# A two-layer hybrid attention trunk on one Trainium2 core: the seven products of a Strassen-Winograd projection in another order, with the loads and epilogues around them moved

## Chip, cores and metric

The kernel runs on one core of one Trainium2 chip. The metric is device microseconds (us) from the first to the last instruction of one execution; the time shown is the median of several runs.

## The reference, cut to what matters

The input x (512 frames of 2048 channels, fp32) gets 16 meta tokens in front: L = 528 positions. One layer of gated differential attention and one layer of gated sliding-window attention follow, then a final norm. The change lies in the first layer:

```python
h = rms_norm(x, norm_g)
q, k, v, gate = jnp.split(h @ w_in, 4, axis=-1)      # w_in: 2048 x 8192
q = partial_rope(q.reshape(B, L, 16, 128), cos, sin)
k = partial_rope(k.reshape(B, L, 16, 128), cos, sin)
...
o = diff_attention(q, k, v, lam, cid)                # 8 heads, block-causal softmax
o = rms_norm(o, subln_g) * (1.0 - lambda_init)
o = o.reshape(B, L, D_MODEL) * jax.nn.silu(gate)
return x + o @ w_out
```

## The kernel before, in words

All tiles hold channels in partitions and positions along the free dimension. fp32 matmuls run as sums of three products of rounded halves: an operand is split into hi (a rounded copy, made by ScalarE) and lo (the rest, made by VectorE), and hi x hi, hi x lo and lo x hi are added in PSUM. `wsplit` (L89) splits a 128 x 1024 weight piece (512 KB), `split4` (L161) a piece of x, scaled by the norm's gain g, which lies in the tile `vec`.

**The projection `h @ w_in`** is made for 64 output tiles of 128 channels, in 32 pairs (`Pair`, L312). Pairs 0 to 2 are plain (`plain`, L387): 192 matmuls of 264 columns each. The other 29 use Strassen-Winograd's scheme on 2 x 2 blocks (two tiles, two halves of the input channels, two halves T of the positions): seven products of 24 matmuls each. `build_forms` (L271) makes the seven right-hand forms f1 to f7 of x once; their left-hand forms are sums of four weight pieces: a, b and d are loaded by SP, and s1 and s3 are loaded by SP and then added to by a second DMA that GpSimd (POOL) issues with accumulation (L326). `ORDER` (L341) is the order of the products, `BANK` (L342) the PSUM tile that each adds into: B (two buffers), C and D (one each). `product` (L360) issues one product and its epilogue: a copy by ScalarE where a group is read for the first time, an addition by VectorE after that. A group that is read and then added to further has to wait for that read. The pair's two results e[0] (tags e0x and e0y in turn) and e[1] (one buffer, tag e1) go on to `finish` (L729): rope or the scale rstd for q and k, then a store to DRAM that POOL issues (L464, L468); for the gate pairs 24 to 31 `finish_gate` (L695): scale, tanh, two products with th and with the attention output read back from DRAM (L705), and a store (L708).

**Attention** of head h is a generator, `heads_attend` (L530), that `tick` advances between the passes of the products by about 0.67 steps a product. `v_rows` (L470) loads one half of a head's v from DRAM (`ldv`, issued on ScalarE's queue, L472) and transposes it on TensorE (tile `Tv`); it runs twice a head. `pv` (L608) multiplies the weights with v.

**The start** (L420 to L430): `x_in` loads x by channel tiles and splits them, `w_in` loads and splits the first four weight pieces, `SumSq` (L228) sums the squares of x for the norm: ScalarE squares, POOL adds. `norm_a` (L256) makes rstd.

**The end of the projection**: `og_in` (L719) loads the gated outputs back (`ldog`) and splits them into og0 to og3, the operands of the out-projection, which begins at 882 us.

The order of each engine's instructions is set by a scheduler (from the order in the text, `tc.high_priority()`, the pools' buffers, and its own model); every engine and every DMA queue then runs its row in that order.

Of the kernel before, what the change touches and what calls it, by code (L numbers as in the profile page):

```python
# [14 lines left out]
D = 2048  # L15
# [28 lines left out]
def trunk(tc, xT, w, vecs, sinks, rope, ident_in, out):  # L44
# [58 lines left out]
    def wunit(m, half, place=None, urgent=True):  # L103

        with tc.high_priority() if urgent else ExitStack():
            raw = wp.tile([128, 1024], F32, tag=f"raw{raws[0] % 3}", name="raw")
            raws[0] += 1
            nc.sync.dma_start(raw, w[m, half])
            return wsplit(raw, place)
# [118 lines left out]
    class SumSq:  # L228


        def __init__(self, n, part, spare):
# [13 lines left out]
    ssx = SumSq(  # L245
        L, lambda i: etmp(("e0y", "rr")[i], f"ssx{i}"), lambda k: ld.tile([128, L], F32, tag="ld", name="sqx")
    )
# [64 lines left out]
    class Pair:  # L312


        def __init__(self, m):
            self.m, self.wr = m, {}
# [24 lines left out]
    ORDER = (1, 5, 6, 2, 7, 3, 4)  # L341
    BANK = {1: "B", 6: "B", 7: "B", 4: "B", 5: "C", 3: "C", 2: "D"}  # L342
# [17 lines left out]
    def product(p, i):  # L360
# [3 lines left out]
        if i in (1, 5, 2):  # L364
            setattr(p, b, bank(b))
        o = getattr(p, b)
        passes(o, x, i, i in (1, 5, 2), True)
# [5 lines left out]
        elif i == 6:  # L373
            act.activation(p.e[0][:, t1], o, AF.Copy, scale=-1.0)  # L374
        elif i == 2:
            add(p.e[0][:, t0])
# [10 lines left out]
    def plain(p, units):  # L387

        for t in range(2):
            o = [bank("B"), bank("BCD"[t + 1])] if t == 0 else [bank("B"), bank("D")]  # L390
# [15 lines left out]
            else:  # L406
                p.e[1] = etmp("e1", "e1")
# [7 lines left out]
    def w_in(t, half):  # L415
        place, tag = Q.get([128, 2, 1024], F32R, f"wu{t}{half}")
        units[t, half] = wunit(t, half, place, False)
# [35 lines left out]
    def finish_qk(p, h, i0):  # L453

        for i, t in enumerate(p.e):
            if i0 + i == 0:
                r = etmp("rr", "rr")
                dve.stream_shuffle(out=r, in_=t, mask=[(j + 16) % 32 for j in range(32)])
                dve.tensor_tensor(out=t, in0=t, in1=CR, op=ALU.mult)
                dve.tensor_tensor(out=r, in0=r, in1=SR, op=ALU.mult)  # L460
                dve.tensor_tensor(out=t, in0=t, in1=r, op=ALU.add)
            else:
                dve.tensor_tensor(out=t, in0=t, in1=rstd, op=ALU.mult)
            pl.dma_start(qkv_dram[h][128 * (i0 + i) : 128 * (i0 + i) + 128], t)  # L464

    def finish_v(p, h):
        for i, t in enumerate(p.e):
            pl.dma_start(qkv_dram[h][512 + 128 * i : 640 + 128 * i], t)  # L468

    def v_rows(h, dt, vq):  # L470
        raw = ld.tile([128, L], F32, tag="ld", name="ldv")
        nc.scalar.dma_start(raw, qkv_dram[h][512 + 128 * dt : 640 + 128 * dt])  # L472
        T = psT.tile([128, 512], F32, tag="T", name="Tv")
# [56 lines left out]
    def heads_attend(h):  # L530
# [98 lines left out]
        if tails:  # L629
            tails.pop()()  # L630
            yield
        v_rows(h, 0, vq)
# [4 lines left out]
        v_rows(h, 1, vq)  # L637
# [5 lines left out]
        pv(0)  # L643
# [3 lines left out]
        yield  # L647
        trows(2)
        yield
# [6 lines left out]
        for _ in pre:  # L656
            yield
        trows(3)
        tmeta(1)
        yield  # L660
        pv(1)
# [33 lines left out]
    def finish_gate(p, j):  # L695
# [3 lines left out]
        for i, z in enumerate(p.e):  # L699
            dve.tensor_tensor(out=z, in0=z, in1=rstd, op=ALU.mult)  # L700
            th = etmp("rr", "th")
            act.activation(th, z, AF.Tanh, scale=0.5)
            dve.scalar_tensor_tensor(out=z, in0=th, scalar=1.0, in1=z, op0=ALU.add, op1=ALU.mult)
            oo = ld.tile([128, L], F32, tag="ld", name="ldo")
            pl.dma_start(oo, o_dram[j][i])  # L705
            pl.tensor_tensor(out=z, in0=z, in1=oo, op=ALU.mult)
            if j < 7:
                pl.dma_start(og_dram[j][i], z)  # L708
            else:
                split_og(14 + i, z)  # L710
# [7 lines left out]

    def og_in(q4):  # L719
# [4 lines left out]
        for m in range(4 * q4, min(4 * q4 + 4, 14)):  # L724
            t = ld.tile([128, L], F32, tag="ld", name="ldog")
            pl.dma_start(t, og_dram[m // 2][m % 2])
            split_og(m, t)

    def finish(j):  # L729
        p = PAIRS[j]  # L730
        made[0] = j + 1
        if j >= 24:
            finish_gate(p, j - 24)
        elif j % 3 < 2:
            finish_qk(p, j // 3, 2 * (j % 3))
        else:
            finish_v(p, j // 3)
            steps.append(heads_attend(j // 3))

    for j in range(PLAIN):  # L740
        plain(PAIRS[j], units if j == 0 else {})
        if j == 0:
            PAIRS[PLAIN].load("s1", "s3")
            Q.free(*wtags)
            building = build_forms()
            for _ in range(5):
                next(building)
            steps.append(building)
            rate[:] = [1.0, 0.0]
        finish(j)  # L750
# [7 lines left out]
    for j in range(PLAIN, 32):  # L758
        p, q = PAIRS[j], PAIRS[j + 1] if j < 31 else None
        if j == 28:  # L760
            drain()
            og_in(0)
        for i in ORDER:
            product(p, i)
# [278 lines left out]
    m = 0  # L1043
# [146 lines left out]
```

## Time and profile before

| | us |
|---|---|
| median of 3 runs (lowest, highest) | 1748.71 (1746.19, 1749.03) |
| the profiled execution, its own time | 1755.2 |
| its span, first to last instruction | 1753.4 |
| busy TensorE (PE), share of the span | 1665.7, 95% |
| busy VectorE (DVE), ScalarE (ACT), GpSimd (POOL) | 1132.1, 866.4, 237.2 |

The span has four stretches: 0 to 96 us, loading and the plain pairs; 96 to 675 us, the pairs of q, k and v with attention between their products; 675 to 882 us, the gate pairs; 882 to 1753 us, everything after the projection (out-projection, second layer), where the text of the kernel is the same before and after. "Busy" of PE counts a matmul from its start to its modelled end; a wait is put down to what released the engine last. The granted clock (PEclk) is 1.00 at 2.4 GHz and 0.50 at 1.2 GHz.

### The profile page before, as it was taken

What the parts mean: (1) busy time and instruction counts of PE and PEld (TensorE: products, weight loads), DVE (VectorE), ACT (ScalarE), POOL (GpSimd) and SP (SyncE); (2) the same over time, 40 slices, a digit from 0 to 9 for tenths busy, and PEclk for the clock granted to TensorE, in tenths of its full rate; (3) what the DMA queues carried; (4) which work ended last, traced back from release to release, by engine and by line L of the source; (5) the groups of instructions that cost most, each with busy time, mean ns of one, the idle gap of its engine ahead of it and who ended that gap; (6) DMA issues with size and microseconds to landing.
All of it is one profiled execution on the core that took longest, in us unless ns stands there. A gap on an engine that the chain in (4) does not pass through costs nothing.

```text
span 1753.4 us, 28723 instructions
## 1 busy us (share of the span) xinstructions
PE 1665.7 (95%) x11383; PEld 1544.2 (88%) x11383; DVE 1132.1 (65%) x1667; ACT 866.4 (49%) x1628; POOL 237.2 (14%) x260
## 2 busy tenths in 40 slices
PE   7899998989999989988899999999999999999996
PEld 7899998989999989988899999888887788888886
DVE  6976777777778767776633337566677777762234
ACT  8565655656566656543522324344545554553331
POOL 3211111111111102243211100010000000000111
PEclk9999999999999999999999999999999999999998
DMA  7367566766676676685644445321222222233332
GB/s 249 113 184 196 161 181 178 189 174 185 186 204 187 169 202 171 182 252 171 209 134 132 141 129 158 131 96 62 84 65 80 73 72 73 69 107 119 120 126 96
DMA packets 83494, 254.81 MB, mean 145 GB/s; under 512 B 10400, under 2 KB 14624, under 8 KB 83360
## 3 DMA queue, kind: packets, MB, share of 16 engines
q1 hardware_dynamic: 47616, 161.25, 27.5%
q0 software_dynamic: 16992, 59.62, 14.8%
q10 hardware_dynamic: 18752, 32.12, 5.9%
q8 instruction: 89, 1.46, 0.3%
q14 instruction: 45, 0.37, 0.1%
HBM read 223.34 MB, written 29.61 MB: 144 GB/s over the span
## 4 chain that ended last, share of the span: by engine, by line
PE 73%; DMA 10%; DVE 8%; ACT 4%; issue 4%; POOL 1%; ACTq 0%; DVEq 0%; SPq 0%; POOLq 0%
PE acc L141 40%; PE B L354 12%; PE C L354 6%; DMA ldv<-qkv_dram 3%; DVE wlo L98 2%; DMA ldqk<-qkv_dram 2%; PE D L354 2%; PE po L616 2%; PE TB L196 1%; PE B L397 1%; DMA ldog<-og_dram 1%; PE poB L983 1%; PE acct L1102 1%; DMA qkv_dram<-e 1%; DMA og_dram<-e 1%
## 5 line engine op out<-in xcount | busy, mean ns | idle before, releaser
L98 DVE TENSOR_TENSOR wlo<-raw,whi 128x1024 fp32r<-128x1024 f32 x140 | 173.7, 1241 | 239.6 <-PE acc L141 187.0
L96 ACT ACTIVATE whi<-raw 128x1024 fp32r<-128x1024 f32 x140 | 148.3, 1060 | 229.0 <-PE acc L141 192.0
L141 PE MATMUL acc<-hh,whi 128*128 128x512 f32 x512 | 202.6, 396 | 0.0
L141 PE MATMUL acc<-hl,whi 128*128 128x512 f32 x512 | 201.0, 392 | 0.0
L141 PE MATMUL acc<-hh,wlo 128*128 128x512 f32 x512 | 129.5, 393 | 0.0
L141 PEld LDWEIGHTS acc<-hh,wlo 128*128 128x128 f32 x512 | 95.9, 188 | 21.8
L141 PEld LDWEIGHTS acc<-hh,whi 128*128 128x128 f32 x512 | 96.3, 188 | 21.1
L141 PEld LDWEIGHTS acc<-hl,whi 128*128 128x128 f32 x512 | 96.4, 188 | 20.5
L326 POOL DMA_DIRECT2D rs<-in_w x58 | 51.9, 894 | 339.8 <-DMA rs<-in_w 166.8
L96 ACT ACTIVATE whi<-rb 128x1024 fp32r<-128x1024 f32 x58 | 61.4, 1059 | 72.4 <-PE B L354 35.8
L243 POOL TENSOR_TENSOR ss<-ss,sq 128x528 f32<-128x528 f32 (+1 forms) x26 | 35.0, 1346 | 445.1 <-ACT sq L242 445.1
L96 ACT ACTIVATE whi<-ra 128x1024 fp32r<-128x1024 f32 x58 | 61.4, 1059 | 58.5 <-PE B L354 29.5
L946 ACT ACTIVATE p<-SB,nm 128x208 f32<-128x208 f32 (+2 forms) x128 | 51.3, 412 | 68.4 <-DVE es L943 61.1
L98 DVE TENSOR_TENSOR wlo<-rb,whi 128x1024 fp32r<-128x1024 f32 x58 | 71.9, 1240 | 16.6 <-PE C L354 8.6
L98 DVE TENSOR_TENSOR wlo<-rs,whi 128x1024 fp32r<-128x1024 f32 x58 | 72.9, 1257 | 9.1 <-PE B L354 6.3
L96 ACT ACTIVATE whi<-rs 128x1024 fp32r<-128x1024 f32 x58 | 61.3, 1056 | 34.7 <-PE C L354 30.9
L354 PE MATMUL C<-f3h,whi 128*128 128x264 f32 x232 | 60.6, 293 | 6.9 <-ACT e L379 6.9
L885 POOL TENSOR_TENSOR qr<-qr,SR 128x512 f32<-128x512 f32 x16 | 22.2, 1390 | 331.7 <-DVE qr L884 264.3
L354 PE MATMUL B<-f7h,whi 128*128 128x264 f32 x232 | 60.1, 293 | 6.0 <-ACT e L374 5.7
L354 PE MATMUL B<-f4h,whi 128*128 128x264 f32 x232 | 64.1, 307 | 0.2
L100 DVE SCALAR_TENSOR_TENSOR wlo<-ra,whi 128x1024 fp32r<-128x1024 f32 x29 | 36.2, 1247 | 42.0 <-PE C L354 29.1
L354 PE MATMUL C<-f5h,whi 128*128 128x264 f32 x232 | 59.7, 291 | 2.9 <-DVE e L369 2.9
(455 smaller groups left out, 5163.0 us busy)
## 6 DMA issues: line engine op xcount, KB each, us to landing
raw<-in_w SPq DMA_DIRECT2D x148, 512.0 KB, 3.3
rs<-in_w SPq DMA_DIRECT2D x58, 512.0 KB, 4.3
rs<-in_w POOLq DMA_DIRECT2D x58, 512.0 KB, 5.8
ra<-in_w SPq DMA_DIRECT2D x29, 512.0 KB, 4.5
rb<-in_w SPq DMA_DIRECT2D x29, 512.0 KB, 4.3
rd<-in_w SPq DMA_DIRECT2D x29, 512.0 KB, 5.7
qkv_dram<-e POOLq DMA_DIRECT2D x48, 264.0 KB, 2.8
hr<-h_dram ACTq DMA_DIRECT2D x32, 256.0 KB, 3.3
```

Of the source, the lines that this page charges most:

```text
L96: act.activation(hi, raw, AF.Copy, scale=sign)
L98: dve.tensor_tensor(out=lo, in0=raw, in1=f(hi), op=ALU.subtract)
L100: dve.scalar_tensor_tensor(out=lo, in0=raw, scalar=sign, in1=f(hi), op0=ALU.mult, op1=ALU.subtract)
L141: pe.matmul(acc[:, s, 0:n], lhsT=a[:, ws], rhs=b[kt // 4][:, kt % 4, c0 : c0 + n], start=(kt == 0 and a is whi and b is hi), stop=(kt == K ...
L196: pe.transpose(o, i, ident[0 : i.shape[0], 0 : i.shape[0]])
L243: pl.tensor_tensor(out=self.acc[i], in0=self.acc[i], in1=t, op=ALU.add)
L326: pl.dma_start(t, w[self.m + 1, 1 if n == "s1" else 0], accum_op=ALU.add)
L354: pe.matmul(o, lhsT=a[:, ws], rhs=b[:, k, :], start=(first and k == 0 and b is fh[i] and a is hi), stop=(last and k == 7 and a is lo), ski ...
L397: pe.matmul(o[s], lhsT=a[:, ws], rhs=b[:, k8, :], start=(half == 0 and k8 == 0 and a is x[0] and b is fh[i]), stop=(half == 1 and k8 == 7 ...
L616: pe.matmul(pov[:, dt, c0:256], lhsT=v_, rhs=w_[:, j, c0:256], start=(j == 0 and k == 0), stop=False)
L885: pl.tensor_tensor(out=r, in0=r, in1=SR[:, META:], op=ALU.mult)
L946: act.activation(p[:, rt, 0:W], Sv[:, rt, :], AF.Exp, bias=nm[:, rt : rt + 1], accum_out=s[:, rt : rt + 1])
```

## The change

The products are issued in the order 1, 5, 2, 6, 3, 4, 7. The fourth starts a PSUM group of its own in D, so that the seventh, now last, adds one result to both halves of e[1]. Each result is finished by itself, e[0] after product 3 and e[1] after product 7. Loads of v are issued one step before their transposes. Gate pairs keep z and the product apart, prefetch the attention output, and the gated outputs are read back into the five places of `po5` some products before they are split. x's loads are issued with high priority, so are the first weight pieces; the adds of x's squares move to VectorE, and the norm (`norm_a`) moves from the first steps of `build_forms` into the second plain pair.

```diff
-    def wunit(m, half, place=None, urgent=True):
+    def wunit(m, half, place=None, raw=None):
-        with tc.high_priority() if urgent else ExitStack():
-            raw = wp.tile([128, 1024], F32, tag=f"raw{raws[0] % 3}", name="raw")
+        with tc.high_priority():
+            if raw is None:
+                raw = wp.tile([128, 1024], F32, tag=f"raw{raws[0] % 3}", name="raw")
...
                 act.activation(t, src, AF.Square)
-                pl.tensor_tensor(out=self.acc[i], in0=self.acc[i], in1=t, op=ALU.add)
+                self.engine.tensor_tensor(out=self.acc[i], in0=self.acc[i], in1=t, op=ALU.add)
...
-            nc.sync.dma_start(x, xT[kt])
+            with tc.high_priority():
+                nc.sync.dma_start(x, xT[kt])
...
-            if kt % 4 == 3:
-                yield
-        norm_a()
-        yield
...
-    ORDER = (1, 5, 6, 2, 7, 3, 4)
-    BANK = {1: "B", 6: "B", 7: "B", 4: "B", 5: "C", 3: "C", 2: "D"}
+    ORDER = (1, 5, 2, 6, 3, 4, 7)
+    BANK = {1: "B", 6: "B", 7: "B", 5: "C", 3: "C", 2: "D", 4: "D"}
...
-        if i in (1, 5, 2):
+        if i in (1, 5, 2, 4):
             setattr(p, b, bank(b))
         o = getattr(p, b)
-        passes(o, x, i, i in (1, 5, 2), True)
+        passes(o, x, i, i in (1, 5, 2, 4), True)
...
-        elif i == 7:
-            add(p.e[1][:, t1])
...
         elif i == 4:
             act.activation(p.e[1][:, t0], o, AF.Copy)
+        else:
+            e = two(p.e[1])
+            dve.tensor_tensor(out=e, in0=o.unsqueeze(1).to_broadcast([128, 2, HALF]), in1=e, op=ALU.add)
...
-        v_rows(h, 0, vq)
+        raw = v_in(h, 0)
         yield
         yield from srows(1)
         trows(0)
         yield
-        v_rows(h, 1, vq)
+        v_rows(raw, 0, vq)
+        raw = v_in(h, 1)
         yield
         trows(1)
         tmeta(0)
         yield from srows(2)
         yield
-        pv(0)
+        v_rows(raw, 1, vq)
         yield
         r3 = srows(3)
         next(r3)
         yield
+        pv(0)
+        yield
...
-            oo = ld.tile([128, L], F32, tag="ld", name="ldo")
-            pl.dma_start(oo, o_dram[j][i])
-            pl.tensor_tensor(out=z, in0=z, in1=oo, op=ALU.mult)
-            if j < 7:
-                pl.dma_start(og_dram[j][i], z)
+        pl.tensor_tensor(out=o, in0=z, in1=o, op=ALU.mult)
+        if j < 7:
+            pl.dma_start(og_dram[j][i], o)
...
+    def og_load(*ms):
+        for m in ms:
+            pl.dma_start(po5[:, m % 5, :], og_dram[m // 2][m % 2])
...
         for i in ORDER:
+            if i == 2 and not steps:
+                gate_in(p, j - 24, 0)
+                gate_in(p, j - 24, 1)
             product(p, i)
+            if i in (3, 7):
+                finish(j, i // 7)
+            if i == 7 and j == 27:
+                drain()
+            elif i == 6 and j == 28:
+                og_load(0, 1, 2, 3)
+            elif i == 6 and j == 29:
+                og_in(0)
+            elif i == 6 and j == 30:
+                og_load(4, 5, 6, 7, 8)
             if q:
-                q.load(*{2: ("a",), 5: ("s1",), 7: ("s3",), 3: ("b",), 4: ("d",)}.get(i, ()))
+                q.load(*{6: ("a",), 5: ("s1",), 7: ("s3",), 3: ("b",), 4: ("d",)}.get(i, ()))
```

### Where the change moves instructions

**SP's queue at the start, before.** The first rows of SyncE's DMA queue: `vec` holds the gains, `xq` and `po` are places of x (264 KB a row), `raw` are weight pieces (512 KB).

```order
L80 DMA vec<-in_vecs 128x70
L252 DMA xq_139<-in_xT 128x528
L108 DMA raw<-in_w 128x1024
L252 DMA xq_139<-in_xT 128x528 x3
L108 DMA raw<-in_w 128x1024
L252 DMA xq_140<-in_xT 128x528 x4
L108 DMA raw<-in_w 128x1024 x2
L252 DMA xq_141<-in_xT 128x528 x4
L108 DMA raw<-in_w 128x1024 x3
```

The same queue with the change, from its fifth row (after four loads of x and two weight pieces in the first four) to `vec`'s.

```order
L255 DMA xq_141<-in_xT 128x528
L109 DMA raw<-in_w 128x1024
L255 DMA po_130<-in_xT 128x528 x2
L109 DMA raw<-in_w 128x1024
L255 DMA po_130<-in_xT 128x528
L109 DMA raw<-in_w 128x1024 x2
L255 DMA po_130<-in_xT 128x528
L109 DMA raw<-in_w 128x1024 x3
L255 DMA xq_139<-in_xT 128x528 x2
L255 DMA xq_140<-in_xT 128x528 x4
L255 DMA xq_141<-in_xT 128x528
L80 DMA vec<-in_vecs 128x70
```

`vec` went from the first row to behind all 16 loads of x and nine weight pieces. Every split of x reads `vec`.

**ACT's queue around the second half of v, head 3.** Before: `ldv` is the load, `vr<-Tv` the first reader of its transposes; whi are hi halves of the next products' weights (4334 for the sixth product, 4363 the second, 4416 the seventh).

```order
L472 DMA ldv_4241<-qkv_dram3_82 128x528
L593 ACTIVATE wh_4172<-T_4174 128x128
L96 ACTIVATE whi_4334<-ra_4074 128x1024
L372 ACTIVATE e0_4268<-B_4224 128x264
L96 ACTIVATE whi_4363<-rb_4179 128x1024
L571 ACT_TABLE_LOAD
L571 ACTIVATE po5_130,s_4156<-S_4157,nm_4155 128x272 x2
L96 ACTIVATE whi_4416<-rs3_4124 128x1024
L385 ACTIVATE e1_3997<-B_3903 128x264
L480 ACTIVATE vr_4250<-Tv_4243,rcol_256 128x128 x4
```

With the change (4375 is for the sixth product, 4418 the third, 4471 the fourth).

```order
L96 ACTIVATE whi_4375<-ra_4085 128x1024
L472 DMA ldv_4193<-qkv_dram3_82 128x528
L509 ACTIVATE po5_130<-po5_130,s_4108 128x272
L371 ACTIVATE e0_4290<-B_4236 128x264
L596 ACTIVATE wh_4124<-T_4253 128x2x128
L607 ACTIVATE wTm_254<-Tm_4258 16x272
L608 ACTIVATE wTm_254<-Tm_4258 16x272
L96 ACTIVATE whi_4418<-rb_4145 128x1024
L96 ACTIVATE whi_4471<-rd_4196 128x1024
L483 ACTIVATE vr_4329<-Tv_4322,rcol_256 128x128 x4
```

On PE, `Tv` stood before right behind the first product of the next pair, and now stands near the end of its second product, with the scores and the fifth product between.

**POOL's queue between two pairs of q and k, head 4.** Before: `rs1` and `rs3` are the accumulating loads of s1 and s3, `e0` and `e1` the results.

```order
L326 DMA rs3_4457<-in_w 128x1024
L464 DMA qkv_dram4_83<-e0_4268 128x528
L464 DMA qkv_dram4_83<-e1_4329 128x528
L326 DMA rs1_4611<-in_w 128x1024
L326 DMA rs3_4740<-in_w 128x1024
```

With the change, the same pair (its results are e0_4290 and e1_4339).

```order
L465 DMA qkv_dram4_83<-e0_4290 128x528
L325 DMA rs3_4556<-in_w 128x1024
L325 DMA rs1_4634<-in_w 128x1024
L465 DMA qkv_dram4_83<-e1_4339 128x528
L671 TENSOR_TENSOR po5_130<-po5_130 128x528
L468 DMA qkv_dram4_83<-e0_4600 128x528
```

The store of the pair's e1 went from ahead of the next s1's accumulation to behind it, and e0's store stands by itself ahead of s3's.

## Rows read from the trace of the kernel before

**Rows 1.** Stretches: length, busy PE, PEld, DVE, ACT, POOL, then granted clock, DMA share, GB/s

```profile
0.00:96.00 96.00, 79.36 (x584) 77.77 (x585) 74.10 (x89) 63.36 (x105) 28.16 (x27) 0.95 0.58 180
96.00:675.00 579.00, 550.02 (x4464) 541.37 (x4463) 423.94 (x629) 345.58 (x670) 78.97 (x105) 0.98 0.65 183
675.00:882.00 207.00, 184.16 (x1426) 180.24 (x1426) 152.08 (x173) 103.70 (x163) 65.15 (x78) 0.97 0.69 204
882.00:1753.00 871.00, 852.12 (x4915) 744.85 (x4914) 481.95 (x777) 353.81 (x692) 64.88 (x51) 0.99 0.32 103
```

**Rows 2.** What PE waited for, 96 to 675 us: us in total, times, longest

```profile
PE Tv L196 <- DMA ldv<-qkv_dram: 18.1, 6, 5.0
PE po L616 <- DVE wl L594: 4.2, 2, 3.6
```

**Rows 3.** The longest of the waits for v: its load's issue, its end, stretches after

```profile
356.20 0.34 ACTq L472 DMA_DIRECT2D ldv<-qkv_dram  x1
...
365.86 0.88 PE L196 MATMUL Tv<-ident,ldv 128*128 128x128 f32 x3 [4.97 <-DMA ldv<-qkv_dram]
...
366.00:370.00 4.00, 4.00 (x19) 4.00 (x20) 0.00 (x0) 0.00 (x0) 0.89 (x1) 0.50 0.31 41
370.00:374.00 4.00, 4.00 (x35) 3.98 (x34) 2.73 (x5) 3.76 (x7) 0.00 (x0) 1.00 0.48 93
```

**Rows 4.** What PE, then ACT, waited for, 675 to 882 us

```profile
PE C L354 <- ACT e L379: 6.9, 4, 3.2
PE B L354 <- ACT e L374: 4.8, 2, 3.8
PE acc L141 <- ACT og3h L716: 3.3, 1, 3.3
PE C L354 <- DVE e L369: 2.9, 1, 2.9
...
ACT e L379 <- DMA og_dram<-e: 17.8, 6, 4.4
ACT og0h L716 <- DMA ldog<-og_dram: 12.3, 3, 6.2
```

**Rows 5.** The start: first matmul, second and third stall, the plain pairs' end (chain)

```profile
7.42 0.59 PE L397 MATMUL B<-f1h,wu 128*128 128x264 f32 x1 [3.93 <-ACT wu L96]
...
28.55 0.53 PE L397 MATMUL B<-f2h,wu 128*128 128x264 f32 x1 [4.38 <-ACT wu L96]
...
56.99 2.13 PE L174 MATMUL ss<-ssx,ones_r 128*128 128x264 f32 x4 [5.03 <-DVE ssx L257]
...
96.54 2.92 PE B L354 x24
```

**Rows 6.** The start: DMA rate, vec's and x's median time to landing, ACT's splits

```profile
2.00:12.00 10.00, 5.14 (x22) 4.79 (x23) 5.85 (x15) 8.16 (x18) 0.00 (x0) 1.00 0.99 348
...
vec<-in_vecs SPq DMA_DIRECT2D x1, 35.0 KB, 1.8
po<-in_xT SPq DMA_DIRECT2D x4, 264.0 KB, 6.9
...
L163 ACT ACTIVATE f1h<-xq,vec x8: 498/503/514, 4.2 to 13.6; 128x264 fp32r<-128x264 f32 x8
```

**Rows 7.** Squares of x: the sum of both halves, and DVE beside POOL's adds

```profile
56.23 0.70 DVE L257 TENSOR_TENSOR ssx<-ssx,ssx 128x528 f32<-128x528 f32 x1
...
43.13 5.05 DVE L285 TENSOR_TENSOR f5l<-xq,f5h 128x1056 fp32r<-128x1056 f32 x1 [3.29 <-ACT f5h L284]
```

**Rows 8.** The s1 load and its accumulation after one pair's fifth product; e1's store

```profile
395.54 0.33 SPq L324 DMA_DIRECT2D rs<-in_w  x1
...
400.17 0.89 POOL L326 DMA_DIRECT2D rs<-in_w  x1 [3.15 <-DMA rs<-in_w]
...
393.55 0.28 PE L354 MATMUL B<-f1h,whi 128*128 128x264 f32 x1
...
qkv_dram<-e POOLq DMA_DIRECT2D x43, 264.0 KB, 2.8
```

More of the change, by code (lines that the diff above doesn't have):

```diff
@@ L228, in trunk, with __init__ @@
     class SumSq:
-        def __init__(self, n, part, spare):
+        def __init__(self, n, part, spare, engine):
+            self.engine = engine
             self.n, self.part, self.spare, self.acc, self.k = n, part, spare, [None, None], 0
@@ L379, in product @@
             act.activation(p.e[1][:, t1], o, AF.Copy, scale=-1.0)
-        elif i == 7:
-            add(p.e[1][:, t1])
+        elif i == 2:
+            add(p.e[0][:, t0])
+        elif i == 6:
+            act.activation(p.e[0][:, t1], o, AF.Copy, scale=-1.0)
         elif i == 3:
@@ L385, in product, with plain @@
             act.activation(p.e[1][:, t0], o, AF.Copy)
-    def plain(p, units):
+        else:
+            e = two(p.e[1])
+            dve.tensor_tensor(out=e, in0=o.unsqueeze(1).to_broadcast([128, 2, HALF]), in1=e, op=ALU.add)
+    def plain(p, units, between):
         for t in range(2):
-            o = [bank("B"), bank("BCD"[t + 1])] if t == 0 else [bank("B"), bank("D")]
+            o = [bank("B"), bank("CD"[t])]
             for half in range(2):
@@ L406, in plain @@
             else:
+                between()
                 p.e[1] = etmp("e1", "e1")
@@ L416, in w_in @@
         place, tag = Q.get([128, 2, 1024], F32R, f"wu{t}{half}")
-        units[t, half] = wunit(t, half, place, False)
+        raw = wx.tile([128, 1024], F32, tag="s1", name="raw") if len(units) == 3 else None
+        units[t, half] = wunit(t, half, place, raw)
         wtags.append(tag)
@@ L451, in trunk, with finish_qk, finish_v, v_in @@
     done = [0]
[L453 to L470, printed above, removed]
+    def finish_qk(t, h, i):
+        if i == 0:
+            r = etmp("rr", "rr")
+            dve.stream_shuffle(out=r, in_=t, mask=[(j + 16) % 32 for j in range(32)])
+            dve.tensor_tensor(out=t, in0=t, in1=CR, op=ALU.mult)
+            dve.tensor_tensor(out=r, in0=r, in1=SR, op=ALU.mult)
+            dve.tensor_tensor(out=t, in0=t, in1=r, op=ALU.add)
+        else:
+            dve.tensor_tensor(out=t, in0=t, in1=rstd, op=ALU.mult)
+        pl.dma_start(qkv_dram[h][128 * i : 128 * i + 128], t)
+    def finish_v(t, h, i):
+        pl.dma_start(qkv_dram[h][512 + 128 * i : 640 + 128 * i], t)
+    def v_in(h, dt):
         raw = ld.tile([128, L], F32, tag="ld", name="ldv")
         nc.scalar.dma_start(raw, qkv_dram[h][512 + 128 * dt : 640 + 128 * dt])
+        return raw
+    def v_rows(raw, dt, vq):
         T = psT.tile([128, 512], F32, tag="T", name="Tv")
@@ L660, in heads_attend @@
         yield
+        for _ in pre:
+            yield
         pv(1)
@@ L724, in og_in, with finish, norm_and_first @@
         for m in range(4 * q4, min(4 * q4 + 4, 14)):
[L725 to L729, printed above, removed]
+            split_og(m, po5[:, m % 5, :])
+    def finish(j, i):
         p = PAIRS[j]
-        made[0] = j + 1
         if j >= 24:
-            finish_gate(p, j - 24)
+            finish_gate(p, j - 24, i)
         elif j % 3 < 2:
-            finish_qk(p, j // 3, 2 * (j % 3))
+            finish_qk(p.e[i], j // 3, 2 * (j % 3) + i)
         else:
-            finish_v(p, j // 3)
-            steps.append(heads_attend(j // 3))
+            finish_v(p.e[i], j // 3, i)
+        if i == 1:
+            made[0] = j + 1
+            if j < 24 and j % 3 == 2:
+                steps.append(heads_attend(j // 3))
+    building = build_forms()
+    def norm_and_first():
+        norm_a()
+        finish(0, 0)
+        finish(0, 1)
     for j in range(PLAIN):
-        plain(PAIRS[j], units if j == 0 else {})
+        plain(PAIRS[j], units if j == 0 else {}, norm_and_first if j == 1 else (lambda: None))
         if j == 0:
@@ L744, in trunk @@
             Q.free(*wtags)
-            building = build_forms()
-            for _ in range(5):
-                next(building)
+            next(building)
             steps.append(building)
             rate[:] = [1.0, 0.0]
-        finish(j)
+        else:
+            finish(j, 0)
+            finish(j, 1)
     for _ in building:
```

51 lines of the change are left out of this document (25 added, 26 removed).

## Prediction

> **What bounds the kernel now.** I read the stretches first [rows 1]. After 882 us nothing of the change runs, and PE is busy for 852 of 871 us: that part stays. Before it PE is idle for 16.6 us in the start, 29.0 in the pairs of q, k and v, and 22.8 in the gate pairs, and its granted clock is below 1.00 there, which costs about (1 - 0.98) x 579 = 11.6 and (1 - 0.97) x 207 = 6.2 us more. Matmuls fill the rest, and the change takes none away. So it can win at most these idle and slow times, and only where it moves what ends a wait.
>
> Next, the list of PE's waits. In the pairs of q, k and v one line holds 18.1 of the 29.0 us: the transposes of v wait for their load, six times [rows 2]. The longest shows how [rows 3]: the load is issued at 356.20, PE wants it at 365.86 - 4.97 = 360.89, and it lands 9.5 us after its issue. After the wait PE does 19 matmuls in 4 us at clock 0.50, where the next 4 us have 35: at 2.92 us for a product's 24 [rows 5], 33 matmuls would be normal, so a long wait costs 14 x 0.122 = 1.7 us more. In the gate pairs PE waits for copies by ACT (6.9 and 4.8 us) and for one addition, and ACT in turn was held by stores of e1 (17.8 us) and by gated outputs that were being read back (12.3 us) [rows 4]. In the start, PE begins at 7.42 us and stalls twice more, 4.4 and 5.0 us; the Winograd pairs begin at 96.5 [rows 5].
>
> **The start: +7 us.** `vec` is now the last of 26 loads: 16 of x and nine weight pieces stand ahead of it, 16 x 264 + 9 x 512 = 8,832 KB or 9.04 MB. The queue moved 348 GB/s between 2 and 12 us [rows 6], so they take 26.0 us, to 28.0. All splits of x read `vec`; one takes ACT 0.50 us [rows 6], I give DVE's half of it the same, so PE begins at 29.0 rather than 7.42. That is 21.6 us later, but most of it comes back, because by then all weights of the first pair are split (they do not read `vec`) and little is left to wait for: the 576 matmuls of the plain pairs take 576 x 0.122 = 70.1 us, the clock's rise 1.7, and the norm's four matmuls, 2.13 us at half clock before [rows 5], 1.1. That ends at 101.9, 5.4 us later than before; I add 1.5 for transposes of the norm and small stalls. Lower bound: `vec` is issued no later than needed if it waits only for the ninth weight piece (2.0 + 7.15 MB / 348 = 22.5) and then takes its 1.8 us from now [rows 6]: +2. Upper bound: both old stalls come again, 9.4 us: +15. I stay near the middle, since a load of x with the queue full took 6.9 us where `vec`, alone, took 1.8 [rows 6]: what stands ahead does hold a load up.
>
> The Trainium skill, "DMA: Bandwidth & Descriptors", section "Queues, rings and completion order", says that each DMA engine takes the descriptors of one queue in ring order. By that rule `vec` cannot pass the x loads ahead of it and the start costs +7; without it, the +2 of the bound. The trace agrees as far as its 6.9 against 1.8 us goes.
>
> The squares' 14 additions go to DVE at 0.70 us each, 9.8 us [rows 7]; DVE is busy for 74 of the 96 us [rows 1]. They lie beside PE's 70 us of plain matmuls: 0 on the path. If that cover went, 9.8 us. In return DVE is no longer slowed by POOL: a split of 1056 columns took 5.05 us beside POOL's additions, where twice the 0.70 us for 528 would be 1.4 [rows 7]. That gain is hidden as well.
>
> **The order of products: 0 by itself.** Each group is now read two products before it is added to again (1 before 6, 6 before 7, 5 before 3), where 6, 7 and 4 had one product between. In the pairs of q, k and v PE hardly waited for such a copy, so nothing is won there; in the gate pairs it is part of the next but one term. Product 4 in D waits for VectorE's reading of product 2, with 6 and 3 (5.8 us) between. The last addition is now 528 columns wide, 0.70 us by the nearest row [rows 7]: at most 29 x 0.70 = 20 us more on DVE, which is idle for a quarter of that stretch; the next pair's first group has B's other buffer, so PE does not wait for it.
>
> **v's loads: -21, and +3 back.** With the change the transposes stand further behind the issue: the lo third of product 1 (1.0 us), six score matmuls (at least 6 x 0.122 = 0.7), product 5 (2.9) and nearly all of product 2 (2.7), 7.3 us where it was 4.7. That is 2.6 us more for each of six waits that were 3.0 on the mean and 5.0 at most: about 4 of 18.1 us stay, 14 go. I count four of the six as long enough to have slowed the clock, 1.7 us each: 7 us. What is late next: `pv`'s first part now follows the second transposes closely, and the copies behind them have to be done before it. PE waited 4.2 us for its operand already [rows 2]; that may go or double, -4 to +4, and I take +3. Sum -18, between -33 (all of 18.1, 11.6 and some of the last) and -5 (9 us, and 4 lost again).
>
> **The gate pairs: -17.** The store now reads the tile of the attention output, so e1 is free about a store earlier; the gated outputs are read back products ahead of their split, so ACT does not stand before them. Of the 6.9 + 4.8 + 2.9 = 14.6 us of waits for copies and the addition I let three quarters go (11), of the clock's 6.2 us 4, of the 3.3 us before the out-projection 2. What stays: the chain from product 7 to POOL's product, one addition longer than before, behind which the next e1 waits. Bounds: -5 and -27.
>
> **Sum.** +7 - 18 - 17 = -28: the profiled execution's 1755.2 becomes 1727, and the median, 6.5 us below it, 1748.7 - 28 = **1721 us**.
>
> **Rivals.**
> 1. *Slower: the third product waits for the store of e1.* In two of three pairs that store now stands behind the next s1's accumulation on POOL. Counted from a pair's first matmul, s1's load is issued at 395.54 - 393.55 = 2.0 us, POOL adds at 6.6 for 0.9, and the store lands 2.8 later, at 10.3 [rows 8]; ACT's copy of product 5 into e1 comes after it, at 10.7; product 3 starts after four products, at 11.7, or later by what attention puts between. Spare: 1 us and more. For it: other loads of s1 need not land in 4.6 us, and ACT stands in its queue meanwhile. Against: attention's matmuls lie between in most such pairs. If the load took 9.5 us, as v's did [rows 3], each of 14 pairs would lose 4 us and 1.7 for the clock: 80 us, 1800 us. It turns the sign from about 2 us a pair, a load of some 6.5 us. Chance 0.08.
> 2. *Waits that only change places.* v's load halved (-9, no clock), the gate pairs halved (-8), the start at +12: -5, 1744 us. For it: 18.1 us of waits hang on how full the DMA engines are, not on the issue alone, and POOL's queue is as long as before. Chance 0.16, half of it beyond -3.5.
> 3. *Everything goes.* Without any wait or slow clock from 96 to 882 us: 29.0 + 11.6 + 22.8 + 6.2 = 70, less the start's 7: 1686 us. Against: waits of many kinds remain in these lists. Chance 0.10 for 1700 or less.
> 4. *x's loads are not first in what counts.* If `vec` is not held up, the start costs 2: 1716 us, inside the forecast.
>
> **How the numbers follow.** The forecast (with rival 4) has 0.66. The range 1700 to 1744 leaves out rivals 1 and 3, 0.18. A measurement can tell 0.2%, 3.5 us, from no change. Faster by more: 0.66, 0.10 and 0.08 of rival 2, 0.84; within: 0.06 of it; slower: rival 1 and the rest of rival 2, 0.10.
>
> **What would show it.** First matmul of the plain pairs at 27 to 31 us, right behind `vec`'s landing, no stall of over 2 us from there to the first product, and that near 103. PE's waits for v's load at 0 to 8 us, granted clock 0.99 from there to the gate pairs; in the gate pairs no ACT wait for a store of a result and under 8 us of PE idle; the stretch behind the out-projection's start unchanged at 871. I am wrong if PE's list shows new waits for copies of product 5 (rival 1) or for v as long as before (rival 2), or if the plain pairs end after 111.

## The result, and the profile after

The change is **slower**: 1763.3 us median of 10 runs (1754.7 to 1772.0) against 1748.4 us of 10 runs of the kernel before; the ratio is 1.0089, with a 95% interval from 1.0063 to 1.0115. The forecast was 1721 us, with a range from 1700 to 1744.

The two profiles alone would hide this: the profiled execution of the change took 1756.0 us (span 1753.7), 7 us under its median, and that of before 1755.2 (span 1753.4), 7 us over its own. A repeat below shows where the spread lies. First the stretches of the changed kernel, with the columns of [rows 1]:

```profile
0.00:96.00 96.00, 64.92 (x501) 64.30 (x502) 68.44 (x99) 59.76 (x98) 3.50 (x10) 1.00 0.48 160
96.00:675.00 579.00, 557.24 (x4548) 549.22 (x4547) 430.17 (x635) 349.38 (x677) 82.34 (x109) 0.98 0.66 186
675.00:882.00 207.00, 181.33 (x1422) 178.02 (x1421) 149.19 (x173) 103.30 (x164) 66.20 (x77) 0.96 0.68 200
882.00:1754.00 872.00, 852.40 (x4918) 745.21 (x4916) 480.32 (x775) 353.48 (x691) 64.28 (x50) 0.99 0.32 103
```

PE does 501 matmuls in the first 96 us instead of 584, and 84 more in the second stretch; the gate stretch did not become shorter, and the last took 872 us, as before. Since work slides over such fixed limits, the table from here on is cut at three matmuls: the first Winograd product, the first of pair 24 (gate), and the first of the out-projection, which the timeline has at 869.3 us in the kernel before (882 was drawn too late ahead of the prediction).

| trace, us | Winograd from | q, k, v pairs | gate pairs | rest |
|---|---|---|---|---|
| before | 96.4 | 565.9 | 207.0 | 884.1 |
| the change | 106.5 | 555.6 | 209.6 | 882.0 |

So in this execution: start +10.1, pairs of q, k and v -10.3, gate pairs +2.6, the rest -2.1. What PE waited for, from 106 to 675 us and (below the first dots) from 675 to 882 us, then what ACT waited for in the same two stretches; total, times, longest, as in [rows 2, 4]:

```profile
PE C L353 <- ACT e L374: 10.6, 5, 3.3
PE po L619 <- DVE wl L597: 5.3, 1, 5.3
...
PE C L353 <- ACT e L374: 13.1, 4, 8.1
PE acc L142 <- DVE e L385: 4.3, 1, 4.3
PE B L353 <- ACT e L378: 3.3, 2, 2.6
...
ACT e L374 <- DMA qkv_dram<-e: 37.1, 14, 7.4
...
ACT e L374 <- POOL ldo L714: 21.0, 6, 8.1
```

The 18.1 us for v's load are gone. In their place stands product 3 (C L353), which waits for ACT's copy of product 5 into e1 (L374), and that waits for the previous e1 to leave: for its store in the pairs of q, k and v, for POOL's product that reads it in the gate pairs. One of these waits as the chain shows it (start, us, what):

```profile
533.61 0.71 DVE e L385
534.32 1.13 DVE wlo L98
535.45 0.90 DVE nm L572
536.35 0.63 DVE e L464
...
537.61 6.44 DMA qkv_dram<-e
544.06 0.02 issue
544.08 0.40 ACT e L374
544.48 0.04 issue
544.52 0.59 PE C L353
```

The next pair's first product began at 526.8, so product 7 ended by then; VectorE's row lets the new wide addition (L385) start at 533.61 only, 6.8 us later, the scale (L464) follows at 536.35, and the store takes 6.44 us to land, where the median before was 2.8 [rows 8]. POOL had issued an accumulating load of 512 KB 2.3 us ahead of it, and waited then for VectorE, not for s1. In another of the five waits, which ends at 338.86, the addition came only 1.7 us after the next pair began (320.82), but the scale waited 5.5 us more behind other work of VectorE's row (the first two lines are of VectorE's timeline, the others of the chain):

```profile
322.53 0.69 DVE L385 TENSOR_TENSOR e<-B,e 128x528 f32<-128x528 f32 x1
328.05 0.70 DVE L464 TENSOR_TENSOR e<-e,rstd 128x528 f32<-128x528 f32 x1
...
329.42 8.62 DMA qkv_dram<-e
...
338.42 0.40 ACT e L374
```

Counted from the next pair's first matmul, the five stores are issued after 8.6 to 14.6 us and land 3.6 to 8.6 us after that. A gate wait has another chain:

```profile
777.31 0.57 POOL rs L325
777.88 0.02 issue
777.91 8.80 DMA og_dram<-ldo
786.70 0.40 issue
787.10 0.54 POOL ldo L701
787.64 0.53 POOL po L729
788.17 0.02 issue
788.19 1.32 POOL ldo L714
789.51 0.02 issue
789.53 0.40 ACT e L374
```

Here POOL's row stops at the early load of the attention output (L701) until the store that still reads that buffer has landed, 8.8 us, and the product that frees e1 (L714) stands behind it.

### The profile page after: what moved, and what is told of

It is laid out like the page before. It is cut to its first block, busy times and chain, and to the rows that moved or that the text cites. A ratio compares the mean times of both kernels' runs of the same rounds, so it can differ in the third digit from the quotient of the medians.

```text
span 1753.7 us, 28681 instructions
## 1 busy us (share of the span) xinstructions
PE 1655.9 (94%) x11383; PEld 1536.8 (88%) x11383; DVE 1128.1 (64%) x1681; ACT 865.9 (49%) x1628; POOL 216.3 (12%) x246
## 4 chain that ended last, share of the span: by engine, by line
PE 76%; DMA 9%; DVE 7%; ACT 3%; issue 3%; POOL 2%; SPq 0%; ACTq 0%; DVEq 0%; POOLq 0%
PE acc L142 41%; PE B L353 8%; PE C L353 8%; PE D L353 6%; DMA qkv_dram<-e 4%; DVE wlo L98 2%; PE B L397 2%; PE TB L197 1%; PE poB L1017 1%; PE acct L1136 1%; DMA rs<-in_w 1%; PE po L619 1%; DMA og_dram<-ldo 1%; PE D L397 1%; DMA raw<-in_w 1%
## 5 line engine op out<-in xcount | busy, mean ns | idle before, releaser
L142 PEld LDWEIGHTS acc<-hh,whi 128*128 128x128 f32 x512 | 96.4, 188 | 21.1
L353 PE MATMUL C<-f3h,whi 128*128 128x264 f32 x232 | 65.8, 312 | 24.4 <-ACT e L374 23.8
L353 PEld LDWEIGHTS C<-f3h,whi 128*128 128x128 f32 x232 | 48.6, 209 | 26.5 <-ACT e L374 25.7
L353 PE MATMUL C<-f3l,whi 128*128 128x264 f32 x232 | 63.8, 305 | 0.0
L353 PE MATMUL B<-f7h,whi 128*128 128x264 f32 x232 | 59.4, 289 | 3.3 <-ACT e L378 3.3
L353 PE MATMUL D<-f4h,whi 128*128 128x264 f32 x232 | 59.7, 291 | 1.7 <-DVE e L368 1.7
```

The source lines that it names most:

```text
L142: pe.matmul(acc[:, s, 0:n], lhsT=a[:, ws], rhs=b[kt // 4][:, kt % 4, c0 : c0 + n], start=(kt == 0 and a is whi and b is hi), stop=(kt == K ...
L353: pe.matmul(o, lhsT=a[:, ws], rhs=b[:, k, :], start=(first and k == 0 and b is fh[i] and a is hi), stop=(last and k == 7 and a is lo), ski ...
```

## The experiments

Medians are us; the brackets hold the ratio to runs of the kernel before on the same chip, and its 95% interval. On the chips of the experiments the kernel before took 1748.0 to 1751.4 us, so two runs of different chips are better compared by their ratios: "by ratios" is the difference of two ratios times 1748 us. Such a difference is good to some 6 us, or 9 where a run has four executions only (rs_spldo, rs_oldgate).

**1. The start: vec first** (a_vec).

```diff
-    nc.sync.dma_start(vec, vecs)
+    with tc.high_priority():
+        nc.sync.dma_start(vec, vecs)
```

> The changed kernel with vec's load issued with high priority too, so that it stands first in SP's queue again; everything else as changed. If the start costs what the trace of the changed kernel shows (first Winograd product at 106.5 us instead of 96.4), this gives back 6 to 12 us: the first matmul before 12 us, the Winograd pairs from 95 to 101 us, 1751 to 1757 us against the changed kernel's 1763. If the start is not where the loss lies (the plain pairs wait for loads of x instead), it stays within 3 us of 1763.

1756.9 (1.0035, 1.0015 to 1.0055): 6.4 us back (9 by ratios), but in the trace the first matmul came no earlier than 24.8 and the Winograd pairs began at 104.8, not at 95 to 101. SP's timeline says why (start, us in all, line, transfer):

```profile
0.75 0.39 SPq L81 DMA_DIRECT2D vec<-in_vecs  x1
1.19 0.89 SPq L110 DMA_DIRECT2D raw<-in_w  x2
2.13 2.22 SPq L256 DMA_DIRECT2D xq<-in_xT  x4
...
18.34 4.47 SPq L256 DMA_DIRECT2D xq<-in_xT  x8
```

and PE's:

```profile
24.79 0.59 PE L398 MATMUL B<-f1h,wu 128*128 128x264 f32 x1 [21.23 <-ACT f1h L165]
```

With high priority the tiles of x no longer come in the order of the text: those of the second half of the channels stand ahead, and eight tiles, among them those that the first matmuls need, come last, from 18.34. So two things came too late: vec, and the tiles of x that are needed first.

**2. e1's place** (a_rot). Results take turns in the three places there are, so that the copy of product 5 takes a place whose store was issued products earlier.

```diff
-            self.e = [etmp("e0x" if self.m % 4 == 0 else "e0y", "e0"), None]
+            self.e = [turn("e0"), None]
...
-            p.e[1] = etmp("e1", "e1")
+            p.e[1] = turn("e1")
...
+    turns = [0]
+    def turn(name):
+        turns[0] += 1
+        return etmp(("e0x", "e1", "e0y")[(turns[0] - 1) % 3], name)
```

(and the same place for e[1] in the plain pairs).

> The changed kernel with the results e0 and e1 taking turns in the same three places (e0x, e1, e0y), so that ACT's copy of product 5 waits for the store of an e0 of the pair before, which is issued four products earlier, and not for that of e1. Theory 1 (product 3 waits for e1's store behind s1's accumulation on POOL): PE's waits of product 3 for ACT's copy, 10.6 us from 106 to 675 us and 13.1 us after, fall to under 5 us together, and with the slow clock behind them 20 to 35 us go: 1728 to 1743 us. Rival (the order of products itself, its fourth PSUM group and the wide last addition, delays the copies): the waits stay as they are, 1760 to 1766 us.

1739.8 (0.9937, 0.9913 to 0.9960): 23.5 us less than the change (27 by ratios), and faster than before. PE's waits for the copy from 108 to 647 us:

```profile
PE C L359 <- ACT e L380: 1.4, 1, 1.4
```

The pairs of q, k and v take 538.8 us, 16.8 less than with the change. The gate pairs take 209.8, as in the change: there the 13.1 us went, and waits for a split, another copy and an addition (5.0, 3.9, 3.7 us the longest) came. So the expectation held for the waits and for the time, but all that was won was won in the pairs of q, k and v.

**3. Both** (a_vecrot).

> Both edits together. If the two causes are separate, their gains add: 1718 to 1735 us, faster than the kernel before by over 0.8 per cent. If the start's gain is swallowed by later waits, it equals the run with the three places alone.

1736.0 (0.9912, 0.9884 to 0.9939): 3.8 us less than with the three places alone, and 1 us above the range. The Winograd pairs begin at 103.4 instead of 107.8, which agrees. Whether the gains of runs 1 and 2 add in full these times can't tell; vec first is only part of the start.

**4. The attention's steps alone, in the kernel before** (b_v).

```diff
-        v_rows(h, 0, vq)
+        raw = v_in(h, 0)
...
-        v_rows(h, 1, vq)
+        v_rows(raw, 0, vq)
+        raw = v_in(h, 1)
...
-        pv(0)
+        v_rows(raw, 1, vq)
...
+        pv(0)
```

(and `yield`s beside them. One step of the change is not in this edit: the loading of the next head's q and k moves there behind the last transposes.)

> The kernel before with only the attention's steps changed: v's loads one step before their transposes, pv's first part two steps later; order of products, start, finish and gate pairs as before. By the prediction's term: 18 us faster, 1727 to 1733 us, PE's waits for v's load at 0 to 8 us instead of 18.1. Rival (the waits only change places, to pv or the scores): 1744 to 1749 us.

1754.7 (1.0037, 1.0014 to 1.0060): slower by a little, neither of the two. The waits for v are gone, and the pairs of q, k and v take 554.8 instead of 565.9. Of what came, PE's two lists (108 to 675 us, then 675 to 870) say:

```profile
PE B L354 <- DVE e L369: 11.9, 8, 1.9
PE po L620 <- DVE wTm L609: 6.9, 5, 2.7
PE po L619 <- DVE wl L597: 5.0, 2, 2.7
...
PE C L354 <- ACT e L379: 12.8, 4, 6.3
PE B L354 <- ACT e L374: 8.1, 3, 5.9
```

Product 4, last in the old order, waits for VectorE's addition of product 7 in the same group, and `pv` waits 11.9 us on its two lines, where it had 4.2 [rows 2] and 3.0. The gate pairs give the rest back, 219.6 us instead of 207.0: ACT waited 31.3 us there for stores that still read e1, where the list of before has 17.8 [rows 4]. Why it waits longer there is not shown.

**5. The old order of products in the changed kernel** (a_oldorder): `ORDER`, `BANK`, the narrow addition and e1's last copy by ACT as before.

> The changed kernel with the order of products and the PSUM groups of before (1, 5, 6, 2, 7, 3, 4; no fourth group, narrow addition for product 7, e1 finished by ACT's copy of product 4), the rest as changed, e1 still in one place. If the new order makes product 3 late (it follows product 5 by two products instead of three, and e1's last addition is VectorE's, behind that engine's row), the waits of product 3 for the copy of product 5 fall from 10.6 us in the pairs of q, k and v to under 3, and the time to 1740 to 1750. If the place of the store on POOL behind s1's accumulation makes it, the waits stay and the time is 1757 to 1766.

1749.3 (0.9998, 0.9978 to 1.0018): 14 us less (16 by ratios), as the first theory has it. Product 3 no longer waits for that copy from 108 to 675 us, but

```profile
PE B L353 <- DVE e L368: 20.3, 11, 2.4
```

shows product 4 waiting as in run 4. The new order removes this wait and makes the other. In the two profiles the pairs of q, k and v are equal, 555.4 us here and 555.6 in the change, and the gate pairs are 7.6 us shorter here; so the old order wins nothing in the pairs of q, k and v that the traces show.

**6. e1's store on ScalarE's queue** (a_actst).

```diff
-        pl.dma_start(qkv_dram[h][128 * i : 128 * i + 128], t)
+        (nc.scalar if i % 2 else pl).dma_start(qkv_dram[h][128 * i : 128 * i + 128], t)
```

(and the same in the stores of v).

> The changed kernel with the stores of e1 of the q, k and v pairs issued on ScalarE's queue instead of POOL's; nothing else. If what stands ahead on POOL's queue (s1's accumulating load) makes the store late or slow (6.4 us to landing in one wait of 3.2 us), product 3 waits under 3 us from 106 to 675 us: 1750 to 1757 us. If VectorE's late addition and scale make it, or ScalarE's own row is held by the issue, the waits stay: 1760 us or more.

1745.8 (0.9982, 0.9960 to 1.0004), 17.5 us less than the change (19 by ratios) and beyond either theory; but the profile, of its slowest execution (1753.3), still has 11.2 us of waits of product 3, while ACT's wait for such stores fell from 36.2 to 16.2 us (106 to 662 us). In the five pairs that wait in the change too, the addition comes as late as there, the store follows only 0.3 to 0.6 us sooner, and it lands in 4.6 to 7.6 us. So the place on POOL's row is not what has these stores issued late; VectorE's row is. Where the 17.5 us come from is not shown.

**7. The best start with the three places** (a_rotstart): x's loads and the first four weight pieces without high priority.

```diff
-            with tc.high_priority():
-                nc.sync.dma_start(x, xT[kt])
+            nc.sync.dma_start(x, xT[kt])
...
-        units[t, half] = wunit(t, half, place, raw)
+        units[t, half] = wunit(t, half, place, raw, False)
```

> The changed kernel with the three places for results in turn, and x's loads and the first four weight pieces without high priority (as before), so that SP's queue begins with vec and the first tiles of x again. If the start's loss is the order of x's loads (with vec first alone the first matmul still came at 24.8 us, since the last tiles of x stood first), the first matmul comes before 9 us, the Winograd pairs begin at 94 to 99 us instead of 107.8, and the time is 1727 to 1733 us. If the early loads were hidden work anyway that now returns as stalls, 1737 us or more.

1724.1 (0.9874, 0.9849 to 0.9899). First matmul at 7.58, Winograd pairs from 94.2 instead of 107.8. The start alone gives 16 us against run 2 by the medians, 11 by ratios and 13.7 in the traces. The profile is of its slowest execution (1734.6; the other five took 1722.9 to 1725.3), so its stages below are some us long. This version is called version 7 from here on.

**8. Control: three places in the kernel before** (b_rot).

> The kernel before with the three places for results in turn, nothing else: a control for the run of the changed kernel with them. If its 24 us are the removal of a wait that the change brought, this stays within 7 us of the kernel before, by the 6.9 us of waits for the copy of product 5 in the gate pairs (1740 to 1750 us). If the places are a gain of their own, 1725 to 1732 us.

1744.9 (0.9987, 0.9965 to 1.0008). That is 2 us by ratios, not clear of zero. So most of the 27 us of run 2 are a loss that the change had brought.

**9. The start alone** (a_start): the edit of 7, e1 in one place.

> The changed kernel with only the start undone (x's loads and the first four weight pieces without high priority), e1 still in one place. If the start's 10 us and e1's waits are separate, the Winograd pairs begin at 94 to 97 us and the time is 1747 to 1755 us. If pairs that begin earlier only wait longer for e1, 1757 us or more.

1751.2 (1.0015, 0.9994 to 1.0035): 12 us less than the change. By ratios, undoing the start gives 13 us, the places 27, and both 38 (run 7): separate losses, as far as medians show. The one profile, of the slowest execution (1757.2), does not show it: there the Winograd pairs begin at 92.3, 14.2 us earlier than in the change, and the pairs of q, k and v and the gate pairs take 9.3 and 6.1 us longer, at granted clocks of 0.97 and 0.94.

**10. The gate pairs.** First their early loads on SP's queue, in the change (a_spldo) and in version 7 (rs_spldo):

```diff
-        pl.dma_start(p.o[i], o_dram[j][i])
+        nc.sync.dma_start(p.o[i], o_dram[j][i])
```

> The changed kernel with the gate pairs' loads of the attention output issued on SP's queue instead of POOL's; nothing else. Theory: in the gate pairs POOL's row stops at such a load until the store that still reads its buffer has landed (8.3 us once), the product that reads e1 stands behind it, and so product 3 waits for the copy of product 5 (13.1 us in four waits). Then these four waits fall to under 4 us and the time by 8 to 15 us, to 1748 to 1755. Rival: e1 is held by the chain from product 7 (scale, tanh, product), or SP's weight loads now stand behind the same store: waits as before or new ones for weights, 1760 us or more.

> The same edit in the version with three places for results and the start of before (1724 us). With the places, e1 is no longer waited for, so what POOL's stop still costs there is a split's and the next loads' delay: 1715 to 1724 us; if SP's weights are held up, 1726 us or more.

1762.8 (1.0088, 1.0060 to 1.0115): no gain, the rival held. ACT's and SP's lists, 663 to 875 us:

```profile
ACT e L374 <- POOL ldo L714: 14.6, 5, 5.5
...
SPq L701 <- DMA og_dram<-ldo: 72.5, 12, 11.5
```

POOL's stop moved to SP, e1 was still held by POOL's product, and PE still waited 15.5 us for the copy of product 5. In version 7 the edit gave 1719.1 (0.9829, 0.9771 to 0.9886), **the lowest median**, 30 us less than before; its interval overlaps that of version 7.

Then the whole epilogue of before in version 7 (rs_oldgate): product written over e, stored from there, all loads just ahead of their use.

> The version with three places and the start of before (1724 us), and the gate pairs' epilogue of before too: product written over e, stored from there, the attention output loaded at the finish, the gated outputs loaded just ahead of their splits. If the gate edits win what the prediction gave them, 10 to 18 us are lost: 1734 to 1742 us. If they only trade one wait on a load or store for another, 1720 to 1728 us, with the gate pairs at 205 to 213 us as in all runs so far.

1723.6 (0.9852, 0.9805 to 0.9900), the same as version 7 within the intervals: the gate edits show no gain there. The stages say where they win and lose: the rest is 3 us longer without them (885.9 against 882.7; 884 to 886 in all traces with the old epilogue, 880 to 883 in all with the new), the gate pairs are shorter (200.1; 205.0 in the version with the lowest median).

**11. The attention's steps of before in version 7** (a_rsoldv): the edit of 4 undone, and with it the step that edit left out.

> The version with three places and the start of before, and the attention's steps of before too (v's loads just ahead of their transposes, pv's first part two steps earlier). If the early loads are worth in the new order what the prediction gave them, 12 to 20 us are lost: 1736 to 1744 us, with waits for v's load of 14 us or more in the pairs of q, k and v. If the early loads only move waits, as they did in the kernel before, 1722 to 1729 us.

1751.6 (1.0012, 0.9987 to 1.0038): 27.5 us lost (24 by ratios), more than either theory, and not at v's loads (2.1 us). PE's list, 96 to 662 us:

```profile
PE po L624 <- DVE wl L602: 12.3, 8, 2.9
PE po L625 <- ACT whi L96: 4.4, 3, 1.6
...
PE po L625 <- DVE wTm L614: 1.4, 1, 1.4
```

It is `pv`, two steps earlier, that waits. With the steps of the change `pv` waits 0.3 us in version 7. The pairs of q, k and v are 23.1 us longer in the trace, of which 11.0 are busy time of PE, for as many matmuls, at a granted clock of 0.98 instead of 0.99.

**12. The change again, for more profiles** (after2, after3, after4).

> The changed kernel unaltered, for a second profile: the one at hand is of an execution 7 us below the median. In a slower one the waits of product 3 for the copy of product 5 should be longer than 10.6 and 13.1 us and their landing times of e1's store longer, the start the same within 2 us (Winograd pairs from 105 to 109 us). If instead the start or the part after 872 us differs, the spread is not e1's.

> The changed kernel unaltered, a third profile. If it falls above 1760 us, the waits of product 3 from 106 to 870 us and the slow clock behind them should make up the difference to the first two profiles, the start within 2 us of 106.5.

> The changed kernel unaltered, a fourth profile, for the same question as the third.

Spans: 1750.4, 1752.1 and 1766.4 us. The last is 12.7 us longer than the first profile, and 12.3 of these lie in the pairs of q, k and v (567.9 us instead of 555.6; 547.0 and 552.0 in the second and third); the start (107.3) is within 1 us, the gate pairs (209.6) are the same. Its wait for the copy of product 5, 106 to 662 us:

```profile
PE C L353 <- ACT e L374: 15.7, 5, 4.6
```

against 10.6, 7.1 and 8.3 in the other three. It is the same five pairs that wait in all four (numbers 7, 11, 14, 19 and 22), and up to the issue of the store they run alike: the addition starts 12.3, 1.7, 1.7, 6.8 and 6.8 us after the next pair's first matmul, the store is issued 2.3, 6.9, 6.9, 4.0 and 4.0 us after that, within 0.1 us. Only the landings differ: the five take 31.9 us together in the first profile, then 28.4, 29.6 and 36.9, and the wait is 21.2 to 21.3 us less than that in each. So the spread of these waits is the spread of the stores' landings. Of the 12.3 us, 5.1 are these waits, and 6.4 are PE's busy time for the same 4345 matmuls (540.3 us instead of 533.8). Where these waits are, the clock falls; 540 to 662 us in the first and in the fourth profile:

```profile
540.00:662.00 122.00, 114.26 (x924) 113.13 (x923) 85.37 (x123) 70.26 (x131) 15.82 (x21) 0.97 0.63 182
...
540.00:662.00 122.00, 113.45 (x889) 112.52 (x889) 86.56 (x129) 69.59 (x134) 15.37 (x21) 0.93 0.64 177
```

The fourth does 35 matmuls fewer at nearly the same busy time. The three places do not end the spread of the times: seven of run 2 lie within 4.5 us, but six of version 7 within 11.6, ten of run 8 within 14.8, and ten of the change within 17.3.

The stages of the runs that carry the argument, cut as in the table above:

| trace, us | Winograd from | q, k, v pairs | gate pairs | rest |
|---|---|---|---|---|
| attention's steps alone (b_v) | 95.1 | 554.8 | 219.6 | 884.3 |
| three places in before (b_rot) | 96.2 | 559.6 | 199.3 | 884.4 |
| the change, old order | 107.2 | 555.4 | 202.0 | 880.4 |
| the change, three places (a_rot) | 107.8 | 538.8 | 209.8 | 882.0 |
| version 7 | 94.2 | 542.8 | 212.6 | 882.7 |
| version 7, attention of before | 95.3 | 565.9 | 206.8 | 881.7 |
| version 7, gate of before | 94.1 | 541.0 | 200.1 | 885.9 |
| lowest median (rs_spldo) | 94.3 | 537.1 | 205.0 | 882.2 |

## Why the prediction was wrong

**The step that failed is "The order of products: 0 by itself"**, with rival 1, given 0.08, as its price: the new order makes product 3 wait for the store of e1, and that cost 23.5 us by run 2 (27 by ratios) where the sum has 0. The sign named for it, new waits for copies of product 5, came. The wait came at another size and by another cause than I had priced. I counted the path of the store on POOL, behind s1's accumulation, and found 1 us to spare in a pair; I did not count the path in front of it, on VectorE. In the wait shown first, the wide addition began 6.8 us after the next pair's first product, and I had put it down as 0.70 us on an engine "idle for a quarter of that stretch". A mean idle share says nothing of when one row of an in-order engine comes up. In the five waits the store was issued 8.6 to 14.6 us after the next pair's first matmul, where I had 7.5, and took 3.6 to 8.6 us to land, where I had 2.8. Run 6, with the store off POOL's row, shows that this row was worth 0.6 us a store at most. I also took four products ahead of product 3 as given, and did not say that there had been five: between product 5 and product 3 stood three, now two. PE shows the wait in 5 pairs of q, k and v, where I counted 14 and 80 us (ACT waited in 14), and in four gate pairs, where another chain holds e1.

**The gate pairs: -17, measured +2.6** in the trace and 0 within 9 us by run 10: the second term that failed. I let go three quarters of the waits because each had its cause removed. They changed places: a store is waited for by the next load into its buffer, on POOL or SP, instead of by ACT, PE is idle for 25.7 us of these pairs, where I forecast under 8, and the gate pairs take 199 to 216 us with either epilogue in all runs but run 4. That was rival 2's mechanism, and I gave it 0.16. Only the 2 us ahead of the out-projection came, in the rest (882.0 instead of 884.1).

**The start: +7, measured +10.1** in the trace and 12.1 in runs (a_start), inside its bounds. The first matmul came at 28.77, forecast 29.0. The chain was right as far as it went: vec was issued at 22.78 and landed 4.9 us later, 1.8 when it stood first [rows 6]. The Trainium skill, "DMA: Bandwidth & Descriptors", section "Queues, rings and completion order", has one queue's descriptors taken in ring order by each engine; these 4.9 us behind x's tiles agree. My own sign for it, 6.9 us against 1.8, had set a load of 264 KB against one of 35 KB. But I read the queue's order for vec only: run 1 showed that the tiles of x needed first had also gone to its end. What the forecast missed besides is 2.5 us for the first 5.2 us of matmuls (22, where 39 fit into the next 5.2), where it has 1.7, and a wait of 2.3 for e1's place in the second plain pair. DVE's square additions cost nothing that shows: with them and the old loads the plain pairs end 2 us earlier (94.2). The split that took 5.05 us beside POOL's additions takes 1.25 us in the change, near the 1.4 forecast.

**v: -18, a size met by another mechanism.** PE's waits for v fell from 18.1 us to 0, as forecast. But that alone did not pay: in the kernel before the steps shorten the pairs of q, k and v by 11.1 us and the whole not at all (run 4). In version 7 undoing them costs 24 us by ratios (run 11), and there hardly by v's load (2.1 us of waits): `pv` waits 18.1 us. So, as far as the waits show, what pays is that `pv` comes two steps later, which I had booked as a cost of 3. Why v's load is waited for so little there is not shown. In the change itself the pairs of q, k and v are between 18.9 us shorter and 2.0 us longer than before in the four profiles. The order of products belongs to this term too: with the old order the same steps make product 4 wait for VectorE, 11.9 and 20.3 us in runs 4 and 5.

Without the wait for e1 the change takes 1739.8 us (run 2): inside the range, but 11 us faster than before by ratios and not 28. What is missing is the gate pairs' 17 us and some of the start, against a little more from the attention's steps. That version 7, at 1724.1, lies near the forecast is luck, since the start of before is put back there.

Not settled: why e1's stores land so differently from one execution to the next; what run 6 shortened; and what bounds the gate pairs.

## What to carry to other kernels

Before moving a product's last reader or writer, write down the whole life of its buffer: last write, its place in that engine's own row, the store's issue and landing, the next write. With one buffer this chain is a wait in hiding; taking turns among the places there are cost no memory and gave 24 us here, and little in the kernel before, where nothing had to be repaired. After a priority is set, read the new order of the queue for every transfer that the first instruction needs, not only for the one that the diff names.

## What the runs showed of the hardware

The stores of results to DRAM (264 KB each, POOL's queue) landed in 2.8 us on the median before the change and in 4.3 to 4.9 us after it, single ones in 8.6 and 8.9 us. The same five stores took 28.4 to 36.9 us together in four executions of one program, in which everything up to their issue ran alike, and the waits behind them differed by the same amounts. Moving them to ScalarE's queue did not make them faster (a median of 5.1 us for those moved). PE's first 5.23 us after 28.77 us of idleness took 22 matmuls at a granted clock that the trace gives as 1.00. Most of these start 0.22 us apart, and 0.12 us apart from 35.5 us on: the row of the clock alone does not show a slow beginning.

```profile
28.77:34.00 5.23, 5.23 (x22) 4.97 (x22) 5.23 (x16) 5.23 (x14) 1.91 (x2) 1.00 0.83 212
34.00:39.20 5.20, 5.20 (x39) 5.20 (x39) 5.20 (x15) 5.20 (x14) 0.00 (x0) 1.00 0.64 121
```
